# Merged products and scores of head pairs in the mixer of a two-layer decoder trunk

## The chip, the cores and the metric

One core of one Trainium2 chip. The metric is the device time of one execution in microseconds, the median of several runs.

## What is computed

Two layers on 256 tokens of width 1024, all in float32. In each layer a mixer runs three kinds of attention side by side on one projection, gates each with SiLU, and projects back; then a cross-attention reads a memory of 256 rows. A final RMSNorm ends it. The three attentions, for a sequence of 256, are:

```python
# block heads ("MoBA"): 6 heads of 64; with 256 tokens only the own block is left
p = softmax(where(t_k <= t_q, q @ k.T * 64 ** -0.5, -inf));  a_o = p @ v
# differential: 4 heads, each with two 32-wide query/key halves, values of 64
a = softmax1 - lam * softmax2;  b_o = rms_norm(a @ v, head_norm_g) * (1 - lam_init)
# stick-breaking: 6 heads of 64, strictly causal
w = exp(log_sigmoid(z) + sum of log(1 - sigmoid(z)) between);  c_o = w @ v
merged = concat(a_o * silu(mg), b_o * silu(dg), c_o * silu(sg));  h = h + merged @ w_out
```

## The kernel before

**Dense products.** Weights come in granules of 128 x 1024 (512 KB). Each is split by `load_next` (L137) into a high part (ScalarE, L150) and a rest (VectorE, L151); five granules are kept ahead. A dense product is three matmuls (high times high, rest times high, high times rest). In `w_stationary` (L365) they have 256 columns and the weights stand in the array, lines 383 to 385; in `t_stationary` (L390) they have 512 columns and the tokens stand, lines 401 to 403. The order of the groups in a layer is W2, W3, W0, M, T0, T3, T2, T1, K, then the output projection O0 and O1 in three parts, then the cross-attention.

**Attention of a pair.** Heads go in pairs. The scores of a block pair are four matmuls on two PSUM banks (`score_banks`, L502), one head on partitions 0 to 63 and one on 64 to 127, each recorded as two instructions. `numerators` (L521) adds the mask and takes the maximum on VectorE (L527), exponentiates on ScalarE (L532). `p_transposed` (L537) transposes a head's probabilities on TensorE (L542) and copies them on ScalarE (L545) to a `pt` tile, of which there are four. The product of probabilities and values is `pv` (L548): the values stand, 64 columns wide, the two heads of a pair write the two halves of one bank, lines 553 (256 columns) and 555 (128 columns), four recorded instructions each. Its result is multiplied into a gate tile on VectorE (L688, L734, L785); the differential one is also squared (L732), transposed and summed for its norm (L738, L739). `split_merged` (L558) splits a gate tile into high part (ScalarE, L163) and rest (VectorE, L164) before O0 and O1 read it.

There are three stick-breaking pairs (in the order 1, 2, 0), two differential ones and three block pairs.

**The order on TensorE** is written out by a planner in Python. Every attention is a generator (`sb` L681, `diff` L709, `moba` L770). It issues a piece, then yields the nanoseconds that the piece is taken to need on TensorE and a wait until the next piece is due. `tick` (L114) is called after every twelve 256-column or six 512-column matmuls of a dense product with 1310 ns; it goes through the jobs in the order they were made, and runs each that is due, until pieces of 1200 ns (`JOB_SHARE`) have been issued in this tick. `finish` (L124) runs what is left of the named jobs. TensorE keeps this order; the order on the other engines is made by a scheduler from program order and priorities. Bank tiles come from a pool of eight.

In both layers the planner puts, in the part that matters here (a dot is one tick):

```
T3 . SBpv1 . . . SBs0 . SBw2 tr0 . SBpv2 tr1 . .
T2 . SBw0 Ds0 . SBpv0 . . . . Dcomb0 Ds1 . .
T1 . Dt00 . . Dt01 Dcomb1 . Dpv0 . . Dsum0 Dt10 . . Dt11
K  . Dpv1 . . Dsum1 . dn0 . . tr1 tr2 . tr1 dn1 .
O0 . Ms0 . Ms1 . Ms2     O1 . Mt00 . Mt01 Mt10 . Mpv0 Mt11 Mt20
O0 . Mpv1 Mt21 . Mpv2    O1 . .      O0 . . .     O1 . . .
```

SB is stick-breaking, D differential, M block heads; s are scores, w weights, t a head's transposes (pair, head), pv a product, tr the transposes of queries and keys, dn the norm of the differential heads. (Layer 0 is shown; in layer 1 SBpv1 comes a tick later.) The part of O0 that comes last multiplies the gate chunks of block pairs 0, 1 and 2, in this order: twelve matmuls of pair 0 first, then per output quarter three of pair 1 and three of pair 2.

Of the kernel before, what the change touches and what calls it, by code (L numbers as in the profile page):

```python
# [11 lines left out]
F32 = mybir.dt.float32  # L12
R = mybir.dt.float32r
I32 = mybir.dt.int32
AF = mybir.ActivationFunctionType
OP = mybir.AluOpType
AX = mybir.AxisListType
# [14 lines left out]
          sq=2560, sk=2944, sv=3328, sg=3712)  # L32
# [26 lines left out]
SB_WAIT, SB_PACE = 8000, 9000  # L59
DIFF_WAIT, DIFF_PACE, COMBINE_WAIT, COMBINE_NEXT = 6500, 8500, 3750, 1700  # L60
MOBA_WAIT, MOBA_PACE, MOBA_NEXT = 5200, 2000, 1100
# [7 lines left out]
MOBA_START, SB_START, DIFF_START = 14350, 1500, 1000  # L69
# [7 lines left out]
class Trunk:  # L77
# [535 lines left out]
    def mixer(self, l):  # L613
        nc = self.nc
        xh, xl, sq, squares = self.x_split(self.h, GAINS["attn"] + 8 * l, "x", self.add, True)
# [23 lines left out]
        t2 = self.now + 10500  # L639
# [11 lines left out]
        outs = self.w_stationary(l, "W0", xs)  # L651
# [8 lines left out]
        a, b = self.mixed(l, "M", xs)  # L660
# [6 lines left out]
        def token(g, name):  # L667
            outs = self.t_stationary(l, g, xs)
            r = A([128, 2, 512], name)
            for t in range(2):  # L670
                nc.scalar.activation(r[:, t, :], outs[t], AF.Copy, scale=col[:, t:t + 1])
            return r

        tok = {}

        def sb_v(h, t):
            if h < 2:
                return tok["t3"][:, t, 384 + 64 * h:448 + 64 * h]
            return sv[:, t, 64 * h - 128:64 * h - 64]

        def sb(c):  # L681
            qk = [x[64 * j:64 * j + 64] for j in range(2) for x in (sqk[c], sqk[3 + c])]
            z = [self.softplus(ps) for ps in self.stick_banks(*qk)]
            yield 1070, SB_WAIT
            w = [self.stick_weights(*x) for x in z]
            yield 1070, PT_WAIT
            o = self.pv(lambda j, t: sb_v(2 * c + j, t), w)
            nc.vector.tensor_tensor(self.gate[5 + c], o, self.gate[5 + c], OP.mult)  # L688
            yield 720, 0

        jobs = [self.job(sb(c), SB_START + SB_PACE * i) for i, c in enumerate((1, 2, 0))]

        def transposed(x, blocks, dst):
            for j in range(0, len(blocks), 2):
# [11 lines left out]
        pm = self.work.tile([128, 8], F32, name="dsum")  # L706
        tj = self.job(transposed(t0, [0, 1, 2, 3], dT), ROPE_WAIT)

        def diff(c):  # L709

            self.finish(tj)
            qk = []
            for s in range(4 * c, 4 * c + 4):
                cb, r = s // 4, 32 * (s % 4)
                qk.append([x[r:r + 32, cb * 256:cb * 256 + 256] for x in dT])
            pr = [self.numerators(ps, 32 ** -0.5) for ps in self.score_quad(qk)]
            yield 1100, DIFF_WAIT
            for j in range(2):
                (p1, r1), (p2, r2) = pr[2 * j:2 * j + 2]
                nc.vector.tensor_scalar(r2, r2, self.lam[:, l:l + 1], None, OP.mult)  # L720
                for t, cc in ((0, slice(0, 128)), (1, slice(128, 384))):
                    nc.vector.tensor_scalar(p2[:, cc], p2[:, cc], r2[:, t:t + 1], None, OP.mult)
                    nc.vector.scalar_tensor_tensor(p1[:, cc], p1[:, cc], r1[:, t:t + 1], p2[:, cc],
                                                   OP.mult, OP.subtract)
            yield 0, COMBINE_WAIT
            pts = []
            for j in range(2):
                pts.append(self.p_transposed(pr[2 * j][0]))
                yield 330, (PT_WAIT if j else COMBINE_NEXT)
            o = self.pv(lambda j, t: tok["t2"][:, t, 256 + 64 * (2 * c + j):320 + 64 * (2 * c + j)], pts)  # L730
            q2 = self.work.tile([128, 256], F32, name="sq")
            nc.scalar.activation(q2, o, AF.Square)  # L732
            g = self.gate[3 + c]
            nc.vector.scalar_tensor_tensor(g, o, self.hg[:, l:l + 1], g, OP.mult, OP.mult)  # L734
            yield 720, 2000
            sums = self.bank()
            for t in range(2):
                nc.tensor.transpose(sums[:, t * 128:t * 128 + 128], q2[:, t * 128:t * 128 + 128], self.ident)  # L738
            nc.vector.tensor_reduce(pm[:, 4 * c:4 * c + 4], sums[:, 0:256].rearrange("p (i d) -> p i d", d=64), AX.X,  # L739
                                    OP.add)  # L740
            yield 220, 0

        def diff_norm():
            self.finish(*dj[:2])
# [12 lines left out]
        tok["t3"] = token("T3", "t3")  # L757

        dj = [self.job(diff(c), DIFF_START + DIFF_PACE * c) for c in range(2)]
        t2 = tok["t2"] = token("T2", "t2")  # L760
        self.rope(t2[:, :, 0:256], 4, 64, 8, 0)
# [6 lines left out]
        blk = lambda i: mT[i // 2][:, (i % 2) * 256:(i % 2) * 256 + 256]  # L768

        def moba(c):  # L770
            self.finish(tj2, tj3)
            qk = [x[64 * j:64 * j + 64] for j in range(2) for x in (blk(c), blk(3 + c))]
            ps = []
            for b in self.score_banks(*qk):
                p, r = self.numerators(b, 0.125)
                for t, cc in ((0, slice(0, 128)), (1, slice(128, 384))):
                    nc.vector.tensor_scalar(p[:, cc], p[:, cc], r[:, t:t + 1], None, OP.mult)
                ps.append(p)
            yield 760, MOBA_WAIT
            pts = []  # L780
            for j in range(2):
                pts.append(self.p_transposed(ps[j]))
                yield 330, (PT_LAST if j else MOBA_NEXT)
            o = self.pv(lambda j, t: tok["t3"][:, t, 64 * (2 * c + j):64 * (2 * c + j) + 64], pts)
            nc.vector.tensor_tensor(self.gate[c], o, self.gate[c], OP.mult)  # L785
            yield 640, 0

        mj = [self.job(moba(c), MOBA_START + MOBA_PACE * c) for c in range(3)]
        dj.append(self.job(diff_norm(), DN_AFTER))
        self.memory_k(l)  # L790
# [3 lines left out]
        outs = [self.chunks4() for _ in range(2)]  # L794
# [263 lines left out]
```

## Time and profile before

| | |
|---|---|
| median of 3 runs | 408.78 us (408.69 to 409.66) |
| the profiled execution | 410.26 us |
| its span, first to last instruction | 408.5 us |
| mean granted TensorE clock | 0.991 |
| busy: TensorE, VectorE, ScalarE | 97%, 77%, 68% of the span |

The span is what the trace shows; some 1.8 us of the execution lie around it. Rows of the timeline give the start, then the duration, both in us, the engine (PE is TensorE's matmul, PEld its weight load, DVE is VectorE, ACT is ScalarE), the line, the operation, what it writes and reads, and a count when like instructions follow one another. Durations of matmuls overlap, since the array is pipelined, so distances between starts tell what one costs. In brackets stands idle time of the engine before the row and what ended it.

### The profile page before, as it was taken

To read this page: it belongs to the slowest core of one execution; us is meant where nothing else is said; L and a number is where in the kernel's file an instruction comes from. 1 tells how busy PE (TensorE), PEld (TensorE's weight loads), DVE (VectorE), ACT (ScalarE), POOL (GpSimd) and SP (SyncE) were. 2 spreads that over 40 slices of the span, in tenths; PEclk is the share of its full clock that TensorE was granted. 3 is DMA by queue.
4 is the path that set the end of the run, shared out by engine and by line. 5 is a ranking of instruction groups with operands and counts; after the bars stand their busy time and mean duration, and the time that the engine had idled before them with its cause. 6 is when DMAs were issued, how large, how long until landed. Compare 5 with 4: busy or idle time off the path is not lost.

```text
span 408.5 us, 7735 instructions
## 1 busy us (share of the span) xinstructions
PE 398.1 (97%) x2819; PEld 358.2 (88%) x2819; DVE 315.4 (77%) x787; ACT 276.7 (68%) x586; POOL 39.8 (10%) x105
## 2 busy tenths in 40 slices
PE   6999999999999999999999999999999999999994
PEld 6899998777789989988999999878778998998983
DVE  3959978869967967979798865786987597696964
ACT  4949868876955666648486943888775476574843
POOL 4488840000000000000000000000000000000000
PEclk9899999999999999999999999999999999999998
DMA  7977594433455333641537765444245423452002
GB/s 209 328 242 267 184 335 154 155 105 113 146 176 187 97 109 112 212 142 52 198 127 260 248 209 198 132 130 142 82 156 186 162 97 112 149 170 88 1 2 103
DMA packets 19478, 64.10 MB, mean 157 GB/s; under 512 B 2544, under 2 KB 3184, under 8 KB 19440
## 3 DMA queue, kind: packets, MB, share of 16 engines
q1 hardware_dynamic: 19440, 63.61, 46.3%
q8 instruction: 22, 0.36, 0.4%
q14 instruction: 16, 0.13, 0.1%
HBM read 62.55 MB, written 1.05 MB: 156 GB/s over the span
## 4 chain that ended last, share of the span: by engine, by line
PE 88%; ACT 5%; DVE 4%; DMA 2%; SPq 1%; issue 0%
PE bank L383 15%; PE bank L385 14%; PE bank L384 14%; PE bank L401 6%; PE bank L403 6%; PE bank L402 6%; PE bank L941 3%; PE bank L553 2%; DMA h<-in_xT_dram 2%; ACT prob L532 2%; PE bank L542 1%; PE bank L876 1%; ACT whi L150 1%; PE bank L470 1%; PE bank L471 1%; PE bank L472 1%
## 5 line engine op out<-in xcount | busy, mean ns | idle before, releaser
L151 DVE TENSOR_TENSOR wlo<-wraw,whi 128x1024 fp32r<-128x1024 f32 (+1 forms) x117 | 136.9, 1177 | 40.1 <-ACT whi L150 39.6
L150 ACT ACTIVATE whi<-wraw 128x1024 fp32r<-128x1024 f32 (+1 forms) x117 | 118.0, 1017 | 48.2 <-PE bank L385 25.0
L383 PE MATMUL bank<-xh,whi 128*128 128x256 f32 x416 | 120.4, 289 | 2.9 <-ACT xh L301 2.9
L385 PE MATMUL bank<-xl,whi 128*128 128x256 f32 x416 | 118.5, 285 | 0.0
L384 PE MATMUL bank<-xh,wlo 128*128 128x256 f32 x416 | 118.3, 284 | 0.0
L383 PEld LDWEIGHTS bank<-xh,whi 128*128 128x128 f32 x416 | 80.3, 193 | 4.5 <-ACT xh L301 3.4
L385 PEld LDWEIGHTS bank<-xl,whi 128*128 128x128 f32 x416 | 80.3, 193 | 0.4 <-DVE xl L302 0.4
L384 PEld LDWEIGHTS bank<-xh,wlo 128*128 128x128 f32 x416 | 80.5, 193 | 0.0
L401 PE MATMUL bank<-whi,xh 128*128 128x512 f32 x128 | 52.2, 408 | 0.0
L403 PE MATMUL bank<-whi,xl 128*128 128x512 f32 x128 | 50.1, 392 | 0.0
L402 PE MATMUL bank<-wlo,xh 128*128 128x512 f32 x128 | 50.1, 391 | 0.0
L532 ACT ACTIVATE prob<-prob,mx 128x128 f32<-128x128 f32 (+1 forms) x56 | 24.7, 443 | 8.9 <-DVE mx L529 8.9
L401 PEld LDWEIGHTS bank<-whi,xh 128*128 128x128 f32 x128 | 24.0, 188 | 6.5 <-issue 2.4
L403 PEld LDWEIGHTS bank<-whi,xl 128*128 128x128 f32 x128 | 24.0, 188 | 5.4
L402 PEld LDWEIGHTS bank<-wlo,xh 128*128 128x128 f32 x128 | 24.1, 188 | 4.1
L301 ACT ACTIVATE xh<-h,gains 128x256 fp32r<-128x256 f32 x32 | 14.6, 497 | 9.7 <-DVE h L297 6.3
L383 PE MATMUL bank<-mh,whi 128*128 128x256 f32 x64 | 18.9, 296 | 0.0
L527 DVE CUSTOM_DVE_ANT_0 prob<-bank,cmask 128x128 f32<-128x128 f32 (+1 forms) x56 | 17.8, 352 | 1.1 <-PE bank L518 0.8
L385 PE MATMUL bank<-ml,whi 128*128 128x256 f32 x64 | 18.1, 282 | 0.0
L384 PE MATMUL bank<-mh,wlo 128*128 128x256 f32 x64 | 18.1, 282 | 0.0
L302 DVE SCALAR_TENSOR_TENSOR xl<-h,gains,xh 128x256 fp32r<-128x256 f32 x32 | 14.4, 481 | 3.2 <-ACT xh L301 3.2
L312 ACT ACTIVATE sq<-h 128x256 f32<-128x256 f32 x28 | 11.4, 409 | 6.6 <-DVE sqacc L313 6.2
(268 smaller groups left out, 775.8 us busy)
## 6 DMA issues: line engine op xcount, KB each, us to landing
wraw<-in_w_dram SPq DMA_DIRECT2D x107, 512.0 KB, 4.1
wraw<-in_w_dram SPq DMA_DIRECT2D x10, 256.0 KB, 5.6
wraw<-in_memT_dram SPq DMA_DIRECT2D x4, 512.0 KB, 4.1
h<-in_xT_dram SPq DMA_DIRECT2D x3, 256.0 KB, 7.4
out_dram<-wraw SPq DMA_DIRECT2D x2, 288.0 KB, 2.2
wraw<-in_gfin_dram SPq DMA_DIRECT2D x1, 512.0 KB, 4.9
out_dram<-wraw SPq DMA_DIRECT2D x2, 224.0 KB, 2.2
h<-in_xT_dram SPq DMA_DIRECT2D x2, 128.0 KB, 3.1
```

The lines of the kernel that those rows point to most:

```text
L150: nc.scalar.activation(hi[:, c], raw[:, c], AF.Copy)
L151: nc.vector.tensor_tensor(lo[:, c], raw[:, c], hi[:, c].bitcast(F32), OP.subtract)
L301: nc.scalar.activation(h, src[k], AF.Copy, scale=g)
L302: nc.vector.scalar_tensor_tensor(lw, src[k], g, h.bitcast(F32), OP.mult, OP.subtract)
L383: nc.tensor.matmul(outs[m], whi[:, kk, c], xh[k], start=k == 0 and m % 2 == 0, stop=False, **kw)
L384: nc.tensor.matmul(outs[m], wlo[:, kk, c], xh[k], start=False, stop=False, **kw)
L385: nc.tensor.matmul(outs[m], whi[:, kk, c], xl[k], start=False, stop=k == n - 1, **kw)
L401: nc.tensor.matmul(outs[t], xh[k][:, c], whi[:, kk, :], start=first, stop=False)
L402: nc.tensor.matmul(outs[t], xh[k][:, c], wlo[:, kk, :], start=False, stop=False)
L403: nc.tensor.matmul(outs[t], xl[k][:, c], whi[:, kk, :], start=False, stop=last)
L527: nc.vector.tensor_tensor_reduce(s[:, c], ps[:, c], self.cmask[:, c], 1.0, -3.0e38, OP.add, OP.max, accum_out=m[:, t:t + 1])
L532: nc.scalar.activation(s[:, c], s[:, c], AF.Exp, bias=m[:, t:t + 1], scale=scale, accum_out=sm[:, t:t + 1])
```

## The change

Where a pair's product was issued as soon as its probabilities were ready, it is now kept in a list, and the products of two pairs are issued one right after the other: stick-breaking pairs 1 and 2 (0 alone), both differential pairs, block pairs 0 and 1 (2 alone). Only then are their results multiplied into the gates. The two differential sums are transposed into one bank and reduced by one instruction. The scores of block pairs 0 and 1 are issued together in the first pair's step, those of pair 2 in its own. The nanoseconds that the pieces yield are changed with them.

```diff
--- before.py
+++ after.py
@@ -678,17 +678,30 @@
                 return tok["t3"][:, t, 384 + 64 * h:448 + 64 * h]
             return sv[:, t, 64 * h - 128:64 * h - 64]
 
-        def sb(c):
+        def together(pending, last, first, then):
+
+            pending.append((first, then))
+            if last:
+                outs = [f() for f, _ in pending]
+                for o, (_, f) in zip(outs, pending):
+                    f(o)
+
+        sbp, dp, mp, mq = [], [], [], {}
+
+        def sb(c, last):
             qk = [x[64 * j:64 * j + 64] for j in range(2) for x in (sqk[c], sqk[3 + c])]
             z = [self.softplus(ps) for ps in self.stick_banks(*qk)]
             yield 1070, SB_WAIT
             w = [self.stick_weights(*x) for x in z]
             yield 1070, PT_WAIT
-            o = self.pv(lambda j, t: sb_v(2 * c + j, t), w)
-            nc.vector.tensor_tensor(self.gate[5 + c], o, self.gate[5 + c], OP.mult)
-            yield 720, 0
-
-        jobs = [self.job(sb(c), SB_START + SB_PACE * i) for i, c in enumerate((1, 2, 0))]
+            together(sbp, last, lambda: self.pv(lambda j, t: sb_v(2 * c + j, t), w),
+                     lambda o: nc.vector.tensor_tensor(self.gate[5 + c], o, self.gate[5 + c], OP.mult))
+            yield 720 * len(sbp) * last, 0
+            if last:
+                sbp.clear()
+
+
+        jobs = [self.job(sb(c, i > 0), SB_START + SB_PACE * i) for i, c in enumerate((1, 2, 0))]
 
         def transposed(x, blocks, dst):
             for j in range(0, len(blocks), 2):
@@ -727,18 +740,30 @@
             for j in range(2):
                 pts.append(self.p_transposed(pr[2 * j][0]))
                 yield 330, (PT_WAIT if j else COMBINE_NEXT)
-            o = self.pv(lambda j, t: tok["t2"][:, t, 256 + 64 * (2 * c + j):320 + 64 * (2 * c + j)], pts)
-            q2 = self.work.tile([128, 256], F32, name="sq")
-            nc.scalar.activation(q2, o, AF.Square)
-            g = self.gate[3 + c]
-            nc.vector.scalar_tensor_tensor(g, o, self.hg[:, l:l + 1], g, OP.mult, OP.mult)
-            yield 720, 2000
+            sq = []
+
+            def gated(o):
+                q2 = self.work.tile([128, 256], F32, name="sq")
+                nc.scalar.activation(q2, o, AF.Square)
+                g = self.gate[3 + len(sq)]
+                nc.vector.scalar_tensor_tensor(g, o, self.hg[:, l:l + 1], g, OP.mult, OP.mult)
+                sq.append(q2)
+
+            dp.append((pts, c))
+            if c == 0:
+                return
+            outs = [self.pv(lambda j, t: tok["t2"][:, t, 256 + 64 * (2 * c + j):320 + 64 * (2 * c + j)], pts)
+                    for pts, c in dp]
+            for o in outs:
+                gated(o)
+            yield 1440, 2600
             sums = self.bank()
-            for t in range(2):
-                nc.tensor.transpose(sums[:, t * 128:t * 128 + 128], q2[:, t * 128:t * 128 + 128], self.ident)
-            nc.vector.tensor_reduce(pm[:, 4 * c:4 * c + 4], sums[:, 0:256].rearrange("p (i d) -> p i d", d=64), AX.X,
-                                    OP.add)
-            yield 220, 0
+            for i, q2 in enumerate(sq):
+                for t in range(2):
+                    nc.tensor.transpose(sums[:, i * 256 + t * 128:i * 256 + t * 128 + 128],
+                                        q2[:, t * 128:t * 128 + 128], self.ident)
+            nc.vector.tensor_reduce(pm, sums.rearrange("p (i d) -> p i d", d=64), AX.X, OP.add)
+            yield 440, 0
 
         def diff_norm():
             self.finish(*dj[:2])
@@ -769,21 +794,28 @@
 
         def moba(c):
             self.finish(tj2, tj3)
-            qk = [x[64 * j:64 * j + 64] for j in range(2) for x in (blk(c), blk(3 + c))]
+            if c != 1:
+
+                for i in ((0, 1), (), (2,))[c]:
+                    qk = [x[64 * j:64 * j + 64] for j in range(2) for x in (blk(i), blk(3 + i))]
+                    mq[i] = self.score_banks(*qk)
             ps = []
-            for b in self.score_banks(*qk):
+            for b in mq[c]:
                 p, r = self.numerators(b, 0.125)
                 for t, cc in ((0, slice(0, 128)), (1, slice(128, 384))):
                     nc.vector.tensor_scalar(p[:, cc], p[:, cc], r[:, t:t + 1], None, OP.mult)
                 ps.append(p)
-            yield 760, MOBA_WAIT
+            yield (1520, 0, 760)[c], MOBA_WAIT
             pts = []
             for j in range(2):
                 pts.append(self.p_transposed(ps[j]))
                 yield 330, (PT_LAST if j else MOBA_NEXT)
-            o = self.pv(lambda j, t: tok["t3"][:, t, 64 * (2 * c + j):64 * (2 * c + j) + 64], pts)
-            nc.vector.tensor_tensor(self.gate[c], o, self.gate[c], OP.mult)
-            yield 640, 0
+            together(mp, c > 0, lambda: self.pv(lambda j, t: tok["t3"][:, t, 64 * (2 * c + j):64 * (2 * c + j) + 64],
+                                                pts),
+                     lambda o: nc.vector.tensor_tensor(self.gate[c], o, self.gate[c], OP.mult))
+            yield 640 * len(mp) * (c > 0), 0
+            if c:
+                mp.clear()
 
         mj = [self.job(moba(c), MOBA_START + MOBA_PACE * c) for c in range(3)]
         dj.append(self.job(diff_norm(), DN_AFTER))
```

## Rows read from the trace of the kernel before

**Rows 1.** The page: busy us of each engine, then the chain that ended last by engine.

```profile
PE 398.1 (97%) x2819; PEld 358.2 (88%) x2819; DVE 315.4 (77%) x787; ACT 276.7 (68%) x586; POOL 39.8 (10%) x105
...
PE 88%; ACT 5%; DVE 4%; DMA 2%; SPq 1%; issue 0%
```

**Rows 2.** Waits of TensorE: who for whom, us in total, times, longest.

```profile
PE bank L383 <- ACT xh L301: 2.9, 2, 2.3
PE bank L988 <- DVE warm L969: 1.2, 1, 1.2
```

**Rows 3.** Timeline of TensorE in K: the second differential product.

```profile
118.80 0.28 PE L385 MATMUL bank<-ml,whi 128*128 128x256 f32 x1
119.01 0.65 PE L553 MATMUL bank<-pt,t 128*64 128x256 f32 x4
119.49 0.39 PE L555 MATMUL bank<-pt,t 128*64 128x128 f32 x4
119.81 0.39 PE L383 MATMUL bank<-mh,whi 128*128 128x256 f32 x1
120.03 0.28 PE L384 MATMUL bank<-mh,wlo 128*128 128x256 f32 x1
120.15 0.28 PE L385 MATMUL bank<-ml,whi 128*128 128x256 f32 x1
```

**Rows 4.** Timeline of TensorE in T1: the first differential product, layer 0.

```profile
108.90 0.39 PE L402 MATMUL bank<-wlo,xh 128*128 128x512 f32 x1
109.13 0.40 PE L403 MATMUL bank<-whi,xl 128*128 128x512 f32 x1
109.46 1.17 PE L553 MATMUL bank<-pt,t 128*64 128x256 f32 x3
...
111.32 0.39 PE L402 MATMUL bank<-wlo,xh 128*128 128x512 f32 x1
```

**Rows 5.** The product of rows 3, what runs at 119.45: its second step alone.

```profile
119.27 0.39 PE L553 MATMUL bank<-pt,t 128*64 128x256 f32 x2
```

**Rows 6.** Timeline of TensorE in O0: the scores of the first block pair.

```profile
133.23 0.28 PE L385 MATMUL bank<-xl,whi 128*128 128x256 f32 x1
133.44 0.37 PE L505 MATMUL bank<-mT,mT 64*128 64x128 f32 x1
...
134.09 0.27 PE L505 MATMUL bank<-mT,mT 64*128 64x128 f32 x1
...
134.52 0.28 PE L384 MATMUL bank<-xh,wlo 128*128 128x256 f32 x1
```

**Rows 7.** Timeline of ScalarE: last copies of transposed probabilities, both differential pairs.

```profile
109.66 0.47 ACT L545 ACTIVATE pt<-bank 128x384 f32<-128x384 f32 x1
...
117.94 0.48 ACT L545 ACTIVATE pt<-bank 128x384 f32<-128x384 f32 x1
```

**Rows 8.** Timeline of TensorE in layer 1, around the first differential product.

```profile
304.78 0.40 PE L403 MATMUL bank<-whi,xl 128*128 128x512 f32 x1
...
306.97 0.39 PE L402 MATMUL bank<-wlo,xh 128*128 128x512 f32 x1
```

**Rows 9.** Timeline of the weight loads in the product of rows 3.

```profile
119.28 0.36 PEld L555 LDWEIGHTS bank<-pt,t 128*64 128x64 f32 x4
```

**Rows 10.** Timeline of VectorE in O0: the last read of a bank of K.

```profile
135.37 0.42 DVE L456 TENSOR_TENSOR xq<-bank,rbcm 128x256 f32<-128x256 f32 x1
```

**Rows 11.** Timeline of TensorE: the matmul after the third block pair's product.

```profile
151.23 0.39 PE L383 MATMUL bank<-xh,whi 128*128 128x256 f32 x1
```

**Rows 12.** Timeline of VectorE behind that product.

```profile
151.34 0.42 DVE L785 TENSOR_TENSOR gate<-bank,gate 128x256 f32<-128x256 f32 x1 [0.81 <-PE bank L555]
152.26 0.43 DVE L164 TENSOR_TENSOR xl<-gate,xh 128x256 fp32r<-128x256 f32 x1 [0.49 <-ACT xh L163]
```

**Rows 13.** Timeline of ScalarE behind that product.

```profile
151.81 0.42 ACT L163 ACTIVATE xh<-gate 128x256 fp32r<-128x256 f32 x1 [1.84 <-DVE gate L785]
```

**Rows 14.** VectorE by line and shape: busy us, mean ns; idle before, and for whom.

```profile
L151 DVE TENSOR_TENSOR wlo<-wraw,whi 128x1024 fp32r<-128x1024 f32 x107 | 130.2, 1222 | 36.5 <-ACT whi L150 36.0
```

## The prediction

> **What bounds the kernel now.** Start with the page's busy times and its chain [rows 1]: TensorE is busy 97% of the span and carries 88% of the chain that ended last, so nearly every instruction put on it or taken off it moves the end. Next, ask whether it waits. The list of TensorE's waits has two lines, 4.1 us together [rows 2], both on work of the opening (warm-up, first split of x). From there on the time is the sum of start-to-start distances on TensorE, and those are read in the timeline, one stretch at a time.
>
> A regular 256-column matmul follows the one before by 0.12 us (120.03 to 120.15) [rows 3], a 512-column one by 0.23 us (108.90 to 109.13) [rows 4]. Around one product of probabilities and values this rhythm breaks: from the last regular matmul at 118.80 to the second one after it at 120.03 are 1.23 us [rows 3]. Two regular distances (0.24) would have passed anyway, so the product costs 0.99 us. Its eight half-width instructions start two by two, one for each head, in four steps. The last step before the 128-column ones takes 0.22 us (119.27 to 119.49) [rows 3, 5]; by their columns the 128-column steps are half that, 0.11. Four steps are 0.66 us; the other 0.33 us are entry (0.21 instead of 0.12 to the first pair, and a slow first step of 0.26, 119.01 to 119.27) and exit (119.49 to 119.81 is 0.32, two steps and 0.10 more; then 0.22 to the next matmul instead of 0.12). So a third of every lone product is the price of changing between whole and split array.
>
> The scores of one block pair show the same: 133.23 to 134.52 is 1.29 us, less 0.24 is 1.05 us, of which first to last start take 0.65 [rows 6].
>
> One product per layer is worse. The first differential one goes from 109.13 to 111.32, 2.19 us; less two distances of 0.23 it costs 1.73, that is 0.74 more than an undisturbed one [rows 3, 4]. Its first weight column group starts at 109.46, while the copy of the second head's transposed probabilities ran on ScalarE from 109.66 for 0.47 us, to 110.13 [rows 7]; so the two heads run one after the other instead of side by side. Layer 1 repeats it: 304.78 to 306.97 is 2.19 again [rows 8].
>
> **The change part by part.** *Three product merges per layer* (stick-breaking pairs 1 and 2, the two differential pairs, block pairs 0 and 1). The instructions stay; one entry and one exit go. If the second product runs on at the step rate it costs 0.66 instead of 0.99: 0.33 each, 0.99 us per layer. Bounds: nothing, if the seam costs as much as an exit and an entry; 0.37, if the steps inside are a little shorter than the rounded 0.22. I take 0.33: the step from the 256- to the 128-column pairs [rows 5] is already a change of weights within a burst and is the nearest row.
>
> The row on the weight load bears on this seam: the loads of the 128-column steps begin at 119.28, while the 256-column matmuls started at 119.27 are still running [rows 5, 9]. So a load inside the burst is hidden. The Trainium skill, "TensorE: Matmul & The Clock Gate", Part 3, says that weight loads overlap running matmuls only when the row groups differ; here all loads use the same 128 rows, and this trace does not agree. By the rule the merged product would pay its loads in the open; it is a rival below.
>
> *One score merge per layer.* The second pair's instructions take between 0.66 (same columns per head as a product) and 0.76 (0.65 first to last start plus a step of 0.11) instead of 1.05 [rows 6]. I take 0.70: 0.35 us per layer, bounds 0.29 to 0.39, zero if the seam drains.
>
> *The stalled differential product* moves from T1 to the merge in K, five ticks later. Its copy is then long done, and the 0.74 us per layer go, unless TensorE waits for something else. What is late next: the merge runs pair 0 first, and pair 1's last copy was ready at 118.42 (117.94 plus 0.48), 0.59 us before its product at 119.01 [rows 3, 7]; pair 0's 0.66 us ahead of it only add to this. Bounds: 0 to 0.74; I take all of it.
>
> *Edits at nothing.* The gate multiplications and squares of a held-back product come in pairs (0.4 us each on VectorE or ScalarE), ticks before their readers. The four sum transposes stay, in one group. By the planner's arithmetic the second `transposed` step of T0 comes a tick later (the merged product before it already holds 1440 ns, over the share of 1200), and the block-head transposes one or two ticks of twelve matmuls; each still has a tick or more before its reader. The differential transposes keep their ticks. Buffers: `pt` has four. The two merges before K use exactly four. In the block heads, pair 2's first copy is the fifth and has to wait on ScalarE for the merged product, about one tick; behind it stand copies and weight splits that are used later, and pair 2's own product follows two ticks later. Banks: the score merge wants four at once, next to two of O0 and, until VectorE's last read from 135.37 to 135.79, one of K [rows 10]: seven of eight. O1's two are first written after pair 2's scores.
>
> *The tail of the block heads* has the thinnest cover. Pair 2's product moves from the end of O0's second part to the end of O1's, directly in front of the last O0 part. Its chain was: next matmul 151.23, gate multiplied 151.34, high split 151.81, low split 152.26 to 152.69 [rows 11 to 13], so the high half is ready 1.0 us and the low half 1.46 us after that matmul. Thirty-nine matmuls covered this, twenty-four of O1 and fifteen of O0; now the fifteen do, since the chunk's first matmul is the sixteenth of O0's last part: 0.22 plus 14 times 0.12 is 1.9 us for the high half, 2.1 for the low. It fits with 0.65 us to spare, and not if a weight split of 1.22 us on VectorE stands in the way [rows 14]. I cost it at nothing, bound 0.6 us per layer.
>
> **Sum.** Per layer 0.99 + 0.35 + 0.74 = 2.08 us, twice is 4.16 us. The profiled execution took 410.26 us (span 408.5), 0.4% above the median of 408.78; the sum makes it 406.1, and the median 404.6. About 0.3% (1.2 us) is what a measurement of this kernel tells from no change.
>
> **Rivals.**
> - *The stall comes back elsewhere.* After the differential stretch TensorE runs ahead of ScalarE and VectorE by 1.7 us more per layer, and a later copy or split ends last. For: that stall itself came from a crowded ScalarE. Against: the margin of 0.59 us just named, and no other wait in the list. Time: only 2.68 us go, 406.1.
> - *The seam is an entry.* The second product again needs 0.09 + 0.05 us to start. Each merge then gives 0.14 less, 1.1 us over eight: 405.7. With the stall back too, 407.2.
> - *Loads in the open.* If the second product waited for each of its four load pairs, at 0.14 (the four loads' 0.36 less the 0.22 between the two pairs) [rows 9], it would cost 0.66 + 0.56 = 1.22, 0.23 more than alone: per layer +0.69 - 0.35 - 0.74 = -0.40, together 408.0, no change. This is the Trainium skill's rule from above; the row of the load speaks against it.
> - *The merge waits for banks* (the change does not do what it says: the burst breaks). If a ninth bank were wanted, TensorE would stand in the score burst from 134.1 to 135.8, 1.7 us per layer: 408.0, no change. My count of seven speaks against it.
> - *Slower: the tail.* If two weight splits on VectorE (2.4 us) and as much on ScalarE stand ahead of pair 2's gate and split, its high half comes 1.0 + 4.8 = 5.8 us after the product, against 1.9 of cover: 3.9 us per layer, 412.4. It decides from a wait of 2.1 us per layer up. Against: a weight granule is due every 24 matmuls, 2.9 us, so two at once are unlikely.
>
> **How the numbers follow.** Forecast 0.64; stall back 0.14; seam an entry 0.10 (with or without the stall); loads in the open 0.03; banks 0.04; tail 0.05. The first three are faster (0.88), the next two no change (0.07), the last slower (0.05). The range: below, all upper bounds (0.37 three times, 0.39, 0.74: 2.24 per layer) give 404.3, and a little for another order on ScalarE, 403.8; above, it takes in the stall and the seam singly, to 406.4. That leaves out the three small cases and part of the double one.
>
> **What would show it.** Right: in the timeline, eight steps follow one another where two products merge, with one 0.21 entry and one 0.10 + 0.10 exit; sixteen score instructions in one burst of about 1.4 us; no product in T1's second part, and no split of the merged differential product into single heads; TensorE's list of waits still 4.1 us. Wrong: a distance of over 0.3 us at the seam between two products; a new line in the list of waits, above all on the high split of the last gate chunk or on a copy to `pt`; a gap in the score burst that ends with VectorE's reads of K.

## The result and the profile after

The changed kernel takes 404.82 us (median of 6 runs, 403.63 to 405.8), the kernel before 408.74 (6 runs, 408.43 to 410.18): ratio 0.9896, interval 0.9875 to 0.9918. The forecast was 404.6 in a range of 403.8 to 406.4.

The profiled execution took 403.74 us, at a mean granted clock of 0.996. Its page, to be held against [rows 1] (the span line, the busy times, the chain by engine):

```profile
span 401.8 us, 7732 instructions
...
PE 393.0 (98%) x2819; PEld 356.7 (89%) x2819; DVE 315.9 (79%) x785; ACT 277.9 (69%) x586; POOL 42.5 (11%) x105
...
PE 93%; DVE 3%; DMA 1%; ACT 1%; SPq 1%; issue 0%
```

TensorE runs the same 2819 instructions in 5.1 us less busy time, of which a part belongs to the opening (last section); VectorE has lost the two reduces of the sums that were joined (787 to 785). The chain runs through TensorE for 93% instead of 88%. TensorE's waits, to be held against [rows 2] (the warm-up stands on another line, the code above it having grown):

```profile
PE bank L383 <- ACT xh L301: 1.4, 2, 1.2
PE bank L1020 <- DVE warm L1001: 1.2, 1, 1.2
```

There is no new line, and the first has shrunk by 1.5 us. That one is no merit of the change: it lies in the opening, ahead of the first line that the change touches. So the two spans, 6.7 us apart, must not be compared whole. A landmark helps: the first matmul of T0, which every kernel here issues ahead of all attention. In before, then after, on TensorE's timeline:

```profile
56.59 0.40 PE L401 MATMUL bank<-whi,xh 128*128 128x512 f32 x1
```

```profile
54.07 0.40 PE L401 MATMUL bank<-whi,xh 128*128 128x512 f32 x1
```

From there to the end of the span are 408.5 - 56.59 = 351.9 us before and 401.8 - 54.07 = 347.7 after: **4.2 us less, where 4.16 were forecast**. The other 2.5 us are the opening's; the last section shows what they are. Below, "from T0 on" is always span less this start.

**The merged product** in K (layer 0, TensorE), where [rows 3] had one pair alone:

```profile
114.05 0.28 PE L385 MATMUL bank<-ml,whi 128*128 128x256 f32 x1
114.26 0.65 PE L553 MATMUL bank<-pt,t 128*64 128x256 f32 x4
114.74 0.39 PE L555 MATMUL bank<-pt,t 128*64 128x128 f32 x4
114.96 0.60 PE L553 MATMUL bank<-pt,t 128*64 128x256 f32 x4
115.39 0.39 PE L555 MATMUL bank<-pt,t 128*64 128x128 f32 x4
115.71 0.39 PE L383 MATMUL bank<-mh,whi 128*128 128x256 f32 x1
115.94 0.28 PE L384 MATMUL bank<-mh,wlo 128*128 128x256 f32 x1
```

From 114.05 to 115.94 are 1.89 us, less two regular distances 1.65, where 1.73 + 0.99 stood before: 1.07 less. The seam is the distance 114.74 to 114.96, 0.22: two 128-column steps and nothing besides. The second product's 256-column rows last 0.60 and not 0.65, as it has no slow first step. The 0.21 of the entry and the 0.32 + 0.23 of the exit are there once.

**The merged scores** in O0 (layer 0, TensorE; the burst's first and last row and the matmuls around it):

```profile
129.36 0.28 PE L385 MATMUL bank<-xl,whi 128*128 128x256 f32 x1
129.57 0.37 PE L505 MATMUL bank<-mT,mT 64*128 64x128 f32 x1
...
130.87 0.27 PE L505 MATMUL bank<-mT,mT 64*128 64x128 f32 x1
...
131.30 0.28 PE L384 MATMUL bank<-xh,wlo 128*128 128x256 f32 x1
```

129.36 to 131.30 is 1.94, less 0.24 is 1.70 for two pairs, where one alone took 1.05 [rows 6]. The second block costs 0.65.

### The profile page after: what moved, and what is told of

Read it like the earlier page. It is cut to its first block, busy times and chain, and to the rows that moved or that the text cites. A ratio compares the mean times of both kernels' runs of the same rounds, so it can differ in the third digit from the quotient of the medians.

```text
span 401.8 us, 7732 instructions
## 1 busy us (share of the span) xinstructions
PE 393.0 (98%) x2819; PEld 356.7 (89%) x2819; DVE 315.9 (79%) x785; ACT 277.9 (69%) x586; POOL 42.5 (11%) x105
## 3 DMA queue, kind: packets, MB, share of 16 engines
HBM read 62.55 MB, written 1.05 MB: 158 GB/s over the span
## 4 chain that ended last, share of the span: by engine, by line
PE 93%; DVE 3%; DMA 1%; ACT 1%; SPq 1%; issue 0%
PE bank L383 15%; PE bank L384 14%; PE bank L385 14%; PE bank L401 8%; PE bank L403 7%; PE bank L402 7%; PE bank L973 3%; PE bank L553 2%; PE bank L542 2%; PE bank L908 1%; DMA h<-in_xT_dram 1%; PE bank L470 1%; PE bank L471 1%; PE bank L472 1%; PE bank L605 1%; PE bank L711 1%
```

## The experiments

All times in us. "Ratio" is against the kernel before, run beside it. One execution's trace gives the last column; by the two executions of the changed kernel (347.7 and 348.0) it is good to a few tenths.

| kernel | median (range) | ratio, interval | from T0 on |
|---|---|---|---|
| before | 408.74 | 1 | 351.9 |
| changed | 404.82 (403.63–405.8) | 0.9896, 0.9875–0.9918 | 347.7 |
| e1 late product | 407.04 (406.39–409.39) | 0.9963, 0.9945–0.9981 | 350.9 |
| e2 seam refilled | 407.17 (406.4–407.19) | 0.9954, 0.9939–0.997 | 350.6 |
| e3 differential part alone | 406.44 (406.14–407.9) | 0.9954, 0.9936–0.9972 | 349.7 |
| e4 block part alone | 407.42 (406.64–408.39) | 0.997, 0.9956–0.9983 | 350.8 |
| e5 three block products | 403.74 (403.32–404.26) | 0.9878, 0.9864–0.9891 | 347.4 |
| e6 also three stick-breaking | 405.2 (404.9–405.53) | 0.9911, 0.9896–0.9926 | 348.6 |
| e7 also three score blocks | 407.11 (407.03–407.96) | 0.9966, 0.9953–0.9978 | 350.9 |
| e8 changed kernel again | 404.69 (403.46–406.13) | 0.9906, 0.989–0.9922 | 348.0 |
| e9 e6 with a later product | 403.2 (402.81–404.19) | 0.9874, 0.986–0.9889 | 346.5 |
| e10 e9 with a later norm | 402.76 (402.39–403.1) | 0.9855, 0.9843–0.9868 | 346.3 |

The theory is that of the prediction: time goes where TensorE changes between whole and split array, and in the one stalled product. Rival: the time comes from somewhere else, or goes into a wait that the change makes.

**e1: is the stall only a matter of when?** Before, with the first differential product a tick later and still alone:

```diff
-                yield 330, (PT_WAIT if j else COMBINE_NEXT)
+                yield 330, (PT_WAIT + 1310 * (c == 0) if j else COMBINE_NEXT)
```

> The kernel before; only the first differential product waits one tick of six matmuls longer, nothing is merged. Theory (a part of the gain is the stall of this product, 0.74 us a layer, and it needs no merge): the lone product costs 0.99 to 1.00 us instead of 1.73 in both layers, and 1.5 us go in all, ratio 0.996. Rival (the stall belongs to the crowded ScalarE and comes back at the next copy): a new wait of about 0.7 us a layer at a later copy of transposed probabilities, and no change of the total.

TensorE in T1, layer 0, to be held against [rows 4]:

```profile
108.31 0.39 PE L403 MATMUL bank<-whi,xl 128*128 128x512 f32 x1
108.62 0.65 PE L553 MATMUL bank<-pt,t 128*64 128x256 f32 x4
...
109.77 0.40 PE L402 MATMUL bank<-wlo,xh 128*128 128x512 f32 x1
```

1.46, less two distances of 0.23, is 1.00 instead of 1.73, in layer 1 as well. So 0.73 per layer is the stall's price, and no merge is needed to save it. In the median 1.5 us were saved; this one trace has 1.0 from T0 on, and its list of waits names 0.2 at a norm (e10 below) that the list of before does not have. The first row of the product shows the mended form at a glance: four like instructions in 0.65 us, while the stalled one had a row of three in 1.17.

**e2: is it the change of array that costs?** The changed kernel with one whole-array transpose (128 columns, into an unused part of the bank) between the two products of each merge, all else as it was:

```diff
+        if whole:
+            nc.tensor.transpose(o[:, 384:512], self.ident, self.ident)
```

> The changed kernel with one whole-array instruction (a 128 by 128 transpose of the identity, into unused columns) between the two products of every merge, six in all; their order and everything else stay. Theory (what a merge saves is a change between split and whole array): a merged pair of products goes from 1.65 us to 0.11 + 2 x 0.99 = 2.1 us, less at most 0.05 for a shared exit; 0.40 to 0.45 us for each of the six, 2.4 to 2.7 us in all. Rival (the gain is from order and buffers, the seam is worth little): only the instruction's own 0.11 us for each, 0.65 us in all.

TensorE in K, layer 0:

```profile
115.00 0.28 PE L385 MATMUL bank<-ml,whi 128*128 128x256 f32 x1
115.21 0.65 PE L553 MATMUL bank<-pt,t 128*64 128x256 f32 x4
115.70 0.39 PE L555 MATMUL bank<-pt,t 128*64 128x128 f32 x4
116.02 0.33 PE L557 MATMUL bank<-ident 128*128 128x128 f32 x1
116.27 0.65 PE L553 MATMUL bank<-pt,t 128*64 128x256 f32 x4
...
117.30 0.28 PE L384 MATMUL bank<-mh,wlo 128*128 128x256 f32 x1
```

115.00 to 117.30 less 0.24 is 2.06 instead of 1.65: 0.41 each, 2.5 for the six merges. The gap 115.70 to 116.02 is the exit (0.32 again, no longer 0.22), and the second product's first row is back at 0.65. The median is 2.35 us above the changed kernel's, though in another series; the ratios, 0.9954 and 0.9896, do not overlap. Some 0.1 of the 0.41 is the transpose's own (six in a row take 0.66 in all, below); the rest is a second exit and entry. Six small transposes in the wrong place undo more than half of the whole gain. This was the sharpest test of the theory, and it stood. What a change consists of it does not say; the loads in the next section show a part of it.

**e3 and e4: does each part bring its own share?** The differential part of the diff alone, and the block part alone, each put on the kernel before.

> The kernel before with the differential part of the change alone. Theory: 0.74 for the stall and 0.33 to 0.35 for the seam, 1.07 to 1.09 us a layer, 2.15 us in all, ratio 0.9947. Rival (stall comes back): 0.7 us in all and a new wait on a copy.

> The kernel before with the block-head part of the change alone (scores of pairs 0 and 1 in one burst, their products in one, the third pair's product in front of the last part of O0). Theory: 0.39 us for the scores and 0.25 to 0.35 for the products a layer, 1.3 to 1.5 us in all, ratio 0.9966, no wait of TensorE behind the third product. Rival (the tail of the block heads has too little cover): a wait on the high split of the third pair's gate of 0.3 us or more a layer, and a total within 0.8 us of before.

In e3's trace each layer has one burst of 1.65 in place of 1.73 and 0.99, 2.15 us in all; ratio 0.9954, about 1.9 us. In e4's each layer has scores of 1.70 and 1.05 and products of 1.65 and 0.99, and the stalled differential product stays at 1.74; ratio 0.997, about 1.2 us. With the stick-breaking part's 0.74 (0.29 and 0.45, below) the three make 3.8 to 3.9 us, as much as the medians give for the whole (in distances of the traces 2.15 + 1.28 + 0.74 = 4.17). So within the intervals, half a microsecond or more each, the parts add, and nothing speaks for one living off another. The stick-breaking part was not run alone.

**e5: does the rate hold for a third product?** The changed kernel with the third block pair's probabilities in a tile of their own, so that all three block products go in one burst, at the place of the lone third one:

```diff
-        pt = self.work.tile([128, 512], F32, name="pt", bufs=4)
+        pt = self.work.tile([128, 384], F32, name="sbe") if own else self.work.tile([128, 512], F32, name="pt", bufs=4)
...
-            together(mp, c > 0, lambda: self.pv(lambda j, t: tok["t3"][:, t, 64 * (2 * c + j):64 * (2 * c + j) + 64],
+            together(mp, c > 1, lambda: self.pv(lambda j, t: tok["t3"][:, t, 64 * (2 * c + j):64 * (2 * c + j) + 64],
```

> The changed kernel, with the products of all three block pairs in one burst; the third pair's copies of transposed probabilities go to tiles that the stick-breaking heads leave unused by then, so that no copy waits for a buffer. Theory: a third product inside a burst costs 0.65 instead of 0.99, 0.34 us a layer, 0.7 us in all on the changed kernel; the first gate's chain starts when its own product ends, so nothing waits. Rival (the tail has too little cover, since all three gates are now multiplied directly in front of the last part of O0): a wait on a high split of 0.3 us or more a layer, and no gain.

TensorE in O1, layer 0:

```profile
146.34 0.28 PE L385 MATMUL bank<-xl,whi 128*128 128x256 f32 x1
146.54 0.65 PE L553 MATMUL bank<-pt,t 128*64 128x256 f32 x4
...
147.90 0.60 PE L553 MATMUL bank<-sbe,t 128*64 128x256 f32 x4
...
148.87 0.28 PE L384 MATMUL bank<-xh,wlo 128*128 128x256 f32 x1
```

2.53 less 0.24 is 2.29, instead of 1.65 + 0.99: the third costs 0.65 too. The ratio is 0.7 us better than the changed kernel's, as forecast, but the intervals overlap, so the gain is shown by the distances and not by the medians. And the tail, now with all three gate chunks late, still shows no wait.

**e6: the same for stick-breaking.** The weights of pair 1, which comes first, go to two tiles of the block heads that are not yet in use, and all three products are issued in the step of the pair that comes last, pair 0:

```diff
+            w = [self.stick_weights(*x, A([128, 512], f"mT{j}") if c == 1 else None) for j, x in enumerate(z)]
...
-        jobs = [self.job(sb(c, i > 0), SB_START + SB_PACE * i) for i, c in enumerate((1, 2, 0))]
+        jobs = [self.job(sb(c, i > 1), SB_START + SB_PACE * i) for i, c in enumerate((1, 2, 0))]
```

> As the one before, and the products of all three stick-breaking pairs in one burst as well; the second pair's weights wait in tiles of the block heads that are not yet used. Theory: another 0.34 us a layer, 1.4 us in all on the changed kernel. Rival: the planner's later ticks bring a wait on a copy or a bank, and the second half of the gain does not come.

It came out 1.5 us slower than e5. TensorE, then ScalarE, at the end of that burst in layer 0:

```profile
90.70 0.40 PE L403 MATMUL bank<-whi,xl 128*128 128x512 f32 x1
...
92.38 1.13 PE L553 MATMUL bank<-pt,t 128*64 128x256 f32 x3
...
94.22 0.40 PE L402 MATMUL bank<-wlo,xh 128*128 128x512 f32 x1
```

```profile
92.56 0.47 ACT L609 ACTIVATE pt<-bank 128x384 f32<-128x384 f32 x1
```

This is the picture of [rows 4 and 7] again: a row of three that lasts 1.13, and a copy of the second head's weights that ends at 93.03, in the middle of the burst. 90.70 to 94.22 less 0.46 is 3.06 us, 0.76 more than the 2.30 of the same burst undisturbed (e9, below), and layer 1 repeats it (284.71 to 288.24). Besides, the pieces yield other nanoseconds, and in layer 0 the first differential scores no longer stand directly behind the weights of pair 0, with which they shared a change of array (some 0.05 us). The merge was sound and its time was not.

**e7: the third score block as well.** e6 with the scores of all three block pairs in one burst:

```diff
-                for i in ((0, 1), (), (2,))[c]:
+                for i in range(3):
...
-            yield (1520, 0, 760)[c], MOBA_WAIT
+            yield (2280, 0, 0)[c], MOBA_WAIT
```

> As the one before, and the scores of all three block pairs in one burst, which takes six banks beside the two of O0. Theory: a third score block inside the burst costs 0.66 instead of 1.05, 0.39 us a layer, 2.1 us in all on the changed kernel. Rival (the banks are too few): TensorE waits in the burst or in front of O1's first matmul until VectorE has read K's last bank or the first pair's scores, for 0.4 us or more a layer, and the step from the kernel before this one is nothing or a loss.

The burst takes 2.36 us, as the theory had it, and waits for no bank. But the kernel is 1.9 us slower than e6. TensorE's waits:

```profile
PE bank L542 <- DVE prob L806: 2.1, 2, 1.1
```

The transposes of the probabilities now wait for VectorE, which scales them: three pairs' numerators come to it at once, and the planner has moved the third pair's transposes forward. Which of the two weighs more was not tried. Neither theory nor rival had named this. Here is the limit of merging: the burst itself goes on gaining, and the work that reads it comes in a heap.

**e8 and e9: e6 with the product later.** The changed kernel once more for comparison, and e6 with the last pair's product 2400 ns later and the yields put back to 720:

```diff
-            yield 1070, PT_WAIT
+            yield 1070, PT_WAIT + 2400 * last
```

> The changed kernel as it is, beside the next two. Every theory expects the ratio of its first timing, 0.9896, within about 0.002.

> The three products of the block heads and the three of the stick-breaking heads in one burst each, but the stick-breaking burst comes a tick later and its pieces give the planner the old nanoseconds, so that the order of the pieces in T3 and T2 is that of the changed kernel. Theory (what was lost with three stick-breaking products in a burst was the wait on the last pair's weights and the order around it, not the seam): 2.30 us for the burst instead of 3.06, no wait on a copy to pt, and 1.3 us less than the changed kernel in all, ratio 0.9865. Rival (a burst of three products is slower by itself): the burst still takes over 2.6 us.

TensorE, the burst of three in layer 0:

```profile
90.26 0.39 PE L403 MATMUL bank<-whi,xl 128*128 128x512 f32 x1
...
91.93 0.60 PE L553 MATMUL bank<-pt,t 128*64 128x256 f32 x4
...
93.02 0.40 PE L402 MATMUL bank<-wlo,xh 128*128 128x512 f32 x1
```

2.76 less 0.46 is 2.30, no step broken. The median is 1.5 us below e8's in the same series, and from T0 on it is 1.5 us too. From T0 on e6 lies 2.1 us above e9, and the two stalled bursts are 1.5 of them; the rest was not followed up. So e6's loss was the moment of issue and the order around it, and nothing in the merge.

**e10: e9 with the norm's transposes later.** In some traces (e1, e2, e5 and e7) TensorE waits 0.2 to 0.3 us in layer 1 for the norm's `rsx` (L353 behind L337).

```diff
-RSTD_WAIT = 4300, 4300
+RSTD_WAIT = 4300, 5610
```

> The one before, and in layer 1 the second half of the mixer's norm a tick of twelve matmuls later. Theory (the small wait of TensorE on the norm's last VectorE step in layer 1 is the next thing that is late): that wait, up to 0.5 us, goes from the list of waits, and the total falls by as much. Rival: the gates behind the norm come too late, and a wait of the same size or more appears in front of W0.

402.76 us is the lowest time of all, 1.4% under the kernel before. Against e9 it is undecided: the ranges meet, and e9's own trace hardly had the wait, so there was little to take away. The rival's wait in front of the next dense product did not come.

## Why the prediction was right

Each sum below is distances of the two traces, per layer. Both layers make 4.18 us; the medians give 3.9, by the interval 3.4 to 5.1.

| term | forecast | layer 0 | layer 1 |
|---|---|---|---|
| stick-breaking merge | 0.33 | 0.29 | 0.45 |
| differential merge and stall | 0.33 + 0.74 | 1.08 | 1.08 |
| block product merge | 0.33 | 0.25 | 0.25 |
| score merge | 0.35 | 0.39 | 0.39 |
| sum | 2.08 | 2.01 | 2.17 |

- **The seam** was right to 0.01: 0.65 instead of 0.66 for a product in a burst. e2 shows the cause, e5 that it holds for a third.
- **Loads.** The weight loads of the merged product in K (PEld, layer 0):

```profile
114.26 0.20 PEld L553 LDWEIGHTS bank<-pt,t 128*64 128x64 f32 x4
...
114.85 0.25 PEld L553 LDWEIGHTS bank<-pt,t 128*64 128x64 f32 x4
...
115.71 0.19 PEld L383 LDWEIGHTS bank<-mh,whi 128*128 128x128 f32 x1 [0.17 <-issue]
```

  The second product's loads begin at 114.85, while the matmuls of 114.74 run, and its first matmul starts one ordinary step behind these. The load is hidden across the seam too. At the two ends of the burst the first load starts together with its matmul, at 114.26 and at 115.71, and not a step ahead of it; in e2 this happens again on both sides of the whole-array transpose (loads at 116.01 and 116.27, matmuls at 116.02 and 116.27). So late loads go with the changes of array in these rows; whether they are their whole price was not tried. The rule that the prediction quoted from the Trainium skill ("TensorE: Matmul & The Clock Gate", Part 3) would have had it in the open; this trace does not agree.
- **The stall** was right in size (0.74; e1 0.73) and in cause: put the same product a tick later, and it is gone. That it would not come back elsewhere was right too: TensorE has no new wait.
- **Scores**: 0.39 instead of 0.35, the upper bound. The second block needs what eight steps need, 0.65, and not the 0.70 that was taken between the bounds.
- **Block products** gave 0.25 and not 0.33. This is the term most mis-sized, and the step that failed is that every lone product was priced by [rows 3]. Before, the first two block products did not stand alone. TensorE in O1, kernel before, layer 0:

```profile
144.49 0.28 PE L385 MATMUL bank<-xl,whi 128*128 128x256 f32 x1
144.69 0.65 PE L553 MATMUL bank<-pt,t 128*64 128x256 f32 x4
...
145.50 0.87 PE L542 MATMUL bank<-ident,prob 128*128 128x128 f32 x6
...
146.33 0.28 PE L384 MATMUL bank<-xh,wlo 128*128 128x256 f32 x1
```

  Product and six transposes together take 1.84 - 0.24 = 1.60. After the change six such transposes stand alone (141.66 to 142.56) and take 0.66, so the product cost 0.94 here and not 0.99: beside the transposes it shared part of its exit. Two such products are 1.88, and merged they are 1.64, 0.24 less (0.25 before rounding). The merge took products away from neighbours with which they already shared something. The second stick-breaking product had such a neighbour too, in both layers: with the four transposes behind it it took 1.40 (83.55 to 85.41 in layer 0), and four alone take 0.44 after the change (84.48 to 85.38), which leaves it about 0.95. This is the main reason why layer 0 gave 0.29. The first one stood behind two transposes of a norm and shared nothing with them: together 1.23 (72.61 to 74.30), the two alone 0.23 after the change. So what is shared lies at the exit, as far as these rows go.
- **A second stall, overlooked.** In layer 1 the first stick-breaking product of the kernel before was late by a little. TensorE, then ScalarE:

```profile
269.66 0.40 PE L403 MATMUL bank<-whi,xl 128*128 128x512 f32 x1
269.99 0.80 PE L553 MATMUL bank<-pt,sv 128*64 128x256 f32 x4
...
271.28 0.40 PE L402 MATMUL bank<-wlo,xh 128*128 128x512 f32 x1
```

```profile
269.58 0.51 ACT L609 ACTIVATE pt<-bank 128x384 f32<-128x384 f32 x1
```

  1.62 less 0.46 is 1.16 instead of 0.99: the copy ended at 270.09, a tenth behind the first matmul. The sign is the row's 0.80 in place of 0.65. In e1, e3 and e4, which leave this product as it was, it is the same: 0.80, 1.15 in all, and a copy that ends a tenth behind the first matmul. This gain (0.16) and the mis-sized term (0.08 in each layer) nearly cancel: layer 0 gave 0.07 less than forecast and layer 1 0.09 more. That the sum came out within 0.02 us is chance.
- **Edits at nothing** were right. The fifth `pt` copy waited 0.63 us on ScalarE (it started at 144.91) and nobody behind it was late. No gap stands in the score burst, so banks were enough.
- **The tail** held. TensorE, VectorE and ScalarE after the third block product, layer 0, to be held against [rows 11 to 13]:

```profile
149.59 0.39 PE L383 MATMUL bank<-xh,whi 128*128 128x256 f32 x1
```

```profile
149.71 0.42 DVE L815 TENSOR_TENSOR gate<-bank,gate 128x256 f32<-128x256 f32 x1 [0.25 <-PE bank L555]
150.62 0.42 DVE L164 TENSOR_TENSOR xl<-gate,xh 128x256 fp32r<-128x256 f32 x1 [0.49 <-ACT xh L163]
```

```profile
150.16 0.42 ACT L163 ACTIVATE xh<-gate 128x256 fp32r<-128x256 f32 x1 [1.58 <-DVE gate L815]
```

  The high half is ready 0.99 us behind the matmul (150.58) and the low half 1.45 (151.04), against 1.9 and 2.1 of cover; the forecast was 1.0 and 1.46. VectorE's weight split of 1.22 us had ended a quarter of a microsecond before the gate's turn (idle 0.25).

The rivals with a wait, with loads in the open and with a broken burst are refuted by these rows; the entry at the seam by the 0.22 at 114.96.

## What to carry to other kernels

Where TensorE alternates between whole-array and split-array matmuls, count the changes and not the instructions: here each one saved is worth about a third of a microsecond (0.25 where the split burst already shares its exit with transposes). Before a merge is judged, look at the copies that feed its last product: e6 and e9 are the same merge, 2.1 us apart from T0 on, and 1.5 of them go because one was issued while ScalarE was still copying. And stop merging where the readers of a burst come in a heap (e7).

## What was not expected of the hardware

**The opening decides between two granted clocks.** The 2.5 us that the profiled execution of before lost ahead of T0 are a wait and what followed it. Stretches of 2 us of the opening (columns: stretch, its length; busy us and instructions of TensorE, its loads, VectorE, ScalarE and GpSimd; granted clock, DMA share, GB/s), before and then after:

```profile
12.00:14.00 2.00, 2.00 (x13) 2.00 (x12) 1.99 (x5) 2.00 (x6) 0.00 (x0) 0.55 0.82 263
14.00:16.00 2.00, 2.00 (x13) 2.00 (x13) 2.00 (x5) 2.00 (x6) 0.27 (x2) 0.60 0.89 287
```

```profile
12.00:14.00 2.00, 1.97 (x17) 1.77 (x16) 2.00 (x5) 2.00 (x6) 0.00 (x0) 1.00 1.16 359
14.00:16.00 2.00, 2.00 (x19) 2.00 (x19) 2.00 (x6) 2.00 (x7) 1.36 (x1) 1.00 0.94 240
```

In before, TensorE had stood idle for 2.27 us until 11.11, waiting for the split of x; then the granted clock was 0.55 and 0.60, near the lower of its two levels (1.2 of 2.4 GHz), and it did 26 matmuls where after did 36. Ten matmuls at the regular 0.12 are 1.2 us, the longer wait is 1.06: 2.3 of the 2.5. In after the same wait was 1.21 us, and the clock stayed at 1.00. The change has no part in this: in e8, the changed kernel again, the wait was 1.85 us, the clock fell to 0.50, and T0 began at 56.17 and not at 54.07. All twelve traces agree: the four whose longest wait for the split of x was 1.53 us (e2), 1.85 (e8), 1.98 (e6) and 2.27 (before) show a stretch near the lower level soon behind it (0.50 in e2 and e6 from 8 to 10 us), and the eight whose longest was 1.21 us or less show none there. What makes that wait longer or shorter (it is behind the first loads) stayed open. For reading: executions of one kernel whose mean clock is 0.991 to 0.994 are mostly the upper end of its range (of the changed kernel 405.8 at 0.991, against 403.63 at 0.998, though another took 405.19 at 0.998), so a single profile is compared from a landmark behind the opening.

**A heap on VectorE moved TensorE in e7** by 1.1 us at a time, in a stretch where it had never waited before: the order that the planner writes is also what keeps the other engines evenly loaded.
